# Modulation weights with outputs on partitions: one multiply-accumulate on VectorE per 128 outputs

## The chip, the cores and the metric

The kernel runs on one core of one Trainium2 chip. The metric is the device time of one execution in microseconds (us). The kernel before has a median of 2834.01 us over three runs, which lie between 2828.8 and 2840.16.

## What is computed

An encoder trunk of two layers over 256 tokens of 2048 features, in f32. A layer is a token mixer and an MLP of width 8192, and both are modulated by a condition vector `c` of 2048 numbers. Mixer 0 is a sparse attention: an indexer scores the keys, the 64 best of each query are kept, and 16 heads attend to them. Mixer 1 is RWKV-7, a recurrence over the tokens. Cut to what matters here:

```python
c_act = silu(c)                                   # [1, 2048]
for i in range(2):
    mod = c_act @ ada_w[i] + ada_b[i]             # [1, 2048] x [2048, 12288]
    sh1, sc1, g1, sh2, sc2, g2 = split(mod, 6)    # parts 0 to 5
    y = mixer[i](rms_norm(x) * (1 + sc1) + sh1)   # 0: sparse attention, 1: RWKV-7
    x = x + g1 * y
    h = rms_norm(x) * (1 + sc2) + sh2
    x = x + g2 * (square(relu(h @ mlp_w1[i])) @ mlp_w2[i])
return rms_norm(x) * final_g
```

The change is in the line of `mod` alone: a product of one row by a matrix of 2048 x 12288, 100.7 MB a layer, two layers.

## The kernel before

Features lie on the 128 partitions and tokens along the free dimension, so a feature tile is 128 x 256, and a value of `mod` is one number per partition. Every large product is made of three TensorE products: `raw` and `more` are loaded chunks of f32 weights; ScalarE casts the high part `whi` (L87), VectorE or GpSimd subtracts it to get the low part `wlo` (L89; which of the two takes a piece goes by a fixed rotation of the phase), and L182, L183 and L184 multiply high by high, high by low, and low by high.

**Phases.** The launch runs in phases that follow each other, each with its own tiles: the first mixer (until about 455 us: the projection until about 142, low-rank norms and indexer keys until 176, indexer scores until 215, the choice of the best keys until 228, heads from 259), the first MLP (503 to 1280 us in its full loop), the projections and the scan of RWKV (until about 2090), and the second MLP (until the end). An MLP is four blocks of 2048 hidden features: 16 hidden tiles, then 16 output tiles that add to `x`, so 32 weight chunks a block, each of 128 x 2048, with 48 products.

**Modulation.** There are 2 layers x 6 parts x 4 = 48 blocks (`ada_block`) of four feature tiles, 512 outputs. A block reads 4 MB as eight loads of 512 KB into the tile `araw`, which has inputs on partitions and outputs along the free dimension, and takes four steps, one for each quarter of the 16 input tiles. A block is of one of two kinds:

- "array" (17 blocks): L215 multiplies on TensorE, with the activated `c` (tile `cact`) as a stationary operand of 32 equal columns; the four input tiles of a step go to four column groups of the array. L228 then transposes the sums from PSUM in blocks of 32 on VectorE.
- "vector" (31 blocks): L217 makes the first product on ScalarE, and L219 adds the other 15 on VectorE, each a multiply by a number per partition and an add over 128 x 512, into the tile `acc`. L228 transposes `acc`, and L233 reduces it to partial sums.

Both end alike: four tiny products on TensorE (L237) sum the partial sums into a PSUM tile `ps_j`, VectorE adds the bias (L240), and for the scales it adds 1 (L242). The result lands in `mod`, four columns a block.

**Where it stands.** Parts 1 and 0 of layer 0 (eight array blocks) are made beside the first projection, since the first mixer can't start its products without them. Parts 2, 3 and 4 of layer 0 follow beside the rest of the mixer: two steps after each of the eight indexer groups (`ADA_INDEX`), six at the choice of keys (`ADA_TOPK`), two a head (`ADA_HEAD`), where the kinds go array, array, vector. Part 5 of layer 0 and five parts of layer 1 are made in the first MLP, 0.8 steps a weight chunk (`t.rate`), and the last part at 0.2 steps a chunk, enqueued for the second MLP. A scheduler orders each engine's instructions after that, by its own estimates, and each engine then works through its queue in order. So where VectorE's step stands in its queue is fixed before the launch.

The names on VectorE in the rows below: L262 ends a norm over tokens (`sm`); L432 is the turning of queries by their positions; L562 and L564 add up the indexer's scores; L616 and L618 choose the keys; L633 adds the mask to a head's logits `lg` and takes their maximum (one instruction with an accumulator, and the reading of it), L639 and L641 scale the softmax, and then TensorE transposes it.

Of the kernel before, what the change touches and what calls it, by code (L numbers as in the profile page):

```python
# [16 lines left out]
P = 128  # L17
# [79 lines left out]
class Trunk:  # L97
    def __init__(s, ctx, tc, io):
# [11 lines left out]
        s.cact = s.fix.tile([P, NF], F32, name="cact")  # L110
# [5 lines left out]
        s.turn, s.kinds, s.ada_kind = 0, "d", "j"  # L116
# [3 lines left out]
    def phase(s, name, a, b, m, w=0, q=0, l=0, g=()):  # L120
        # the working tiles of a phase: A of 2 KB and B of 1 KB a partition, split weights in pieces, modulation
# [33 lines left out]
    # weights: a chunk of up to 2048 columns, split exactly in two parts  # L155
    def raw(s, ap, own=True):
        if not own and s.bufs["m"]:
            t = s.tp.tile([P, 1024], F32, name="araw", bufs=s.bufs["m"])
        else:
            s.raws += 1  # L160
            if s.raws % (NRAW + s.bufs["q"]) < NRAW:
                t = s.wp.tile([P, 512], F32, name="raw", bufs=NRAW)[:, :ap.shape[-1]]
            else:
                t = s.tp.tile([P, 512], F32, name="more", bufs=s.bufs["q"])[:, :ap.shape[-1]]
        s.nc.sync.dma_start(t, ap)
        return t
# [32 lines left out]
    # modulation: c_act @ ada_w, four feature tiles at a time  # L199
    def ada_block(s, layer, part, j, where):  # L200
        # where the products are made: in the array, on VectorE, or on ScalarE and GpSimd
        nc = s.nc
        blk = part * 4 + j
        array = where == "array"
        if array:
            # partial sums in the four column tiles of the array
            p = s.bank(s.ada_kind)
        acc = None if array else s.tp.tile([P, 512], F32, name="acc", bufs=1 + (s.bufs["m"] > 2))
# [1023 lines left out]
```

## Time and profile before

| | before |
|---|---|
| device time, median of 3 runs | 2834.01 us (2828.8 to 2840.16) |
| span of the profiled execution | 2835.9 us |
| TensorE products busy | 2666.8 us (94%) |
| TensorE weight loads busy | 2460.3 us (87%) |
| VectorE busy | 2009.3 us (71%) |
| ScalarE busy | 1330.1 us (47%) |
| GpSimd busy | 1252.3 us (44%) |
| moved by DMA | 621.70 MB, mean 219 GB/s |

One execution was profiled; its span is the time from its first to its last instruction, and lies 1.9 us above the median of the runs and inside their spread. Busy shares are means over all phases. In the rows further below, PE is TensorE's products, PEld its weight loads, DVE VectorE, ACT ScalarE, POOL GpSimd, SP the engine that issues most DMAs. "x" is a count of instructions. PEclk is the granted clock of TensorE as a share of its full 2.4 GHz.

### The profile page before, as it was taken

Reading aid. Unit: us, or ns where it says so; the run is one execution under the profiler, and the core shown is the slowest. Engines: PE = TensorE matmul, PEld = TensorE weight load, DVE = VectorE, ACT = ScalarE, POOL = GpSimd, SP = SyncE. Lnnn points to the kernel's source line nnn. Section 1 sums busy time; section 2 is a strip of 40 time slices with the busy share of each in tenths; the row PEclk is TensorE's granted clock in tenths of the full one; section 3 lists DMA queues with packets and bytes.
Section 4 is the critical chain, followed back from the end, with each engine's and each line's share of the span. In section 5 each row is a group of like instructions: output and inputs, shape, how many; then the busy total and the mean of one; then the engine's idle time right before and its main releaser. Section 6 shows DMA issues by size and latency. Waiting matters only on the chain. (4 is left out here: it accounts for less than half of the span.)

```text
span 2835.9 us, 65852 instructions
## 1 busy us (share of the span) xinstructions
PE 2666.8 (94%) x25132; PEld 2460.3 (87%) x25132; DVE 2009.3 (71%) x3475; ACT 1330.1 (47%) x2879; POOL 1252.3 (44%) x1121
## 2 busy tenths in 40 slices
PE   7989998899999999998989899999898999999998
PEld 4566688899999999997978788888798999999998
DVE  2276658999999999948887656766798264473653
ACT  3334345445444544446655334444445454454553
POOL 1343237445454454455665412323554444444443
PEclk9998999999999999999999879999999999999999
DMA  9987836999899899854657632333577656555563
GB/s 356 367 305 289 297 106 197 299 312 332 290 302 318 291 312 318 268 174 127 201 174 224 190 91 77 105 113 89 157 262 239 193 182 183 182 182 185 182 182 115
DMA packets 290847, 621.70 MB, mean 219 GB/s; under 512 B 32353, under 2 KB 46049, under 8 KB 290529
## 3 DMA queue, kind: packets, MB, share of 16 engines
q1 hardware_dynamic: 283616, 604.89, 66.0%
q10 hardware_dynamic: 6912, 12.59, 1.2%
q8 instruction: 197, 3.23, 0.5%
q14 instruction: 122, 0.99, 0.1%
HBM read 600.57 MB, written 16.78 MB: 218 GB/s over the span
## 5 line engine op out<-in xcount | busy, mean ns | idle before, releaser
L89 POOL TENSOR_TENSOR wlo<-raw,whi 128x512 fp32r<-128x512 f32 x364 | 515.9, 1423 | 616.5 <-ACT whi L87 439.3
L87 ACT CAST whi<-raw 128x512 fp32r<-128x512 f32 x856 | 516.4, 617 | 453.5 <-PE ps_d L183 158.7
L89 DVE TENSOR_TENSOR wlo<-raw,whi 128x512 fp32r<-128x512 f32 x492 | 412.5, 842 | 236.2 <-ACT whi L87 226.4
L219 DVE SCALAR_TENSOR_TENSOR acc<-araw,cact,acc 128x512 f32<-128x512 f32 x465 | 476.2, 1025 | 8.1 <-ACT acc L217 4.4
L89 POOL TENSOR_TENSOR wlo<-more,whi 128x512 fp32r<-128x512 f32 x181 | 256.0, 1416 | 312.8 <-ACT whi L87 201.2
L87 ACT CAST whi<-more 128x512 fp32r<-128x512 f32 x366 | 223.2, 617 | 218.6 <-PE ps_d L183 75.5
L182 PE MATMUL ps_d<-A,whi 128*128 128x256 f32 x1058 | 312.7, 297 | 12.4 <-ACT B L849 4.6
L183 PE MATMUL ps_d<-A,whi 128*128 128x256 f32 x1058 | 306.1, 290 | 5.7 <-DVE A L196 5.1
L184 PE MATMUL ps_d<-A,wlo 128*128 128x256 f32 x1058 | 303.8, 287 | 0.0
L89 DVE TENSOR_TENSOR wlo<-more,whi 128x512 fp32r<-128x512 f32 (+1 forms) x185 | 152.1, 824 | 141.9 <-ACT whi L87 139.3
L182 PEld LDWEIGHTS ps_d<-A,whi 128*128 128x128 f32 x1058 | 206.0, 195 | 33.3 <-issue 6.5
L183 PEld LDWEIGHTS ps_d<-A,whi 128*128 128x128 f32 x1058 | 206.9, 196 | 10.4 <-DVE A L196 9.0
L184 PEld LDWEIGHTS ps_d<-A,wlo 128*128 128x128 f32 x1058 | 206.5, 195 | 1.4 <-issue 1.4
L183 PE MATMUL ps_d<-h,whi 128*128 128x258 f32 x552 | 157.9, 286 | 2.9 <-DVE h L352 2.8
L184 PE MATMUL ps_d<-h,wlo 128*128 128x258 f32 x552 | 156.8, 284 | 1.9 <-DVE wlo L89 1.9
L182 PE MATMUL ps_d<-h,whi 128*128 128x258 f32 x552 | 157.7, 286 | 0.0
L371 ACT ACTIVATE B<-B,sm 128x256 f32<-128x256 f32 x128 | 65.0, 508 | 197.1 <-DVE B L370 197.0
L182 PE MATMUL ps_m<-h,whi 128*128 128x258 f32 x536 | 153.2, 286 | 0.0
L183 PE MATMUL ps_m<-h,whi 128*128 128x258 f32 x536 | 152.6, 285 | 0.0
L184 PE MATMUL ps_m<-h,wlo 128*128 128x258 f32 x536 | 151.6, 283 | 0.0
L182 PE MATMUL ps_m<-A,whi 128*128 128x256 f32 x510 | 145.6, 286 | 5.4 <-DVE B L372 4.4
L183 PE MATMUL ps_m<-A,whi 128*128 128x256 f32 x510 | 145.0, 284 | 1.5 <-DVE A L375 1.5
(555 smaller groups left out, 8753.1 us busy)
## 6 DMA issues: line engine op xcount, KB each, us to landing
araw<-ada_w_in SPq DMA_DIRECT2D x384, 512.0 KB, 6.3
raw<-mlp_w_in SPq DMA_DIRECT2D x614, 256.0 KB, 4.0
more<-mlp_w_in SPq DMA_DIRECT2D x410, 256.0 KB, 4.2
raw<-b_w_r_in SPq DMA_DIRECT2D x64, 256.0 KB, 3.6
raw<-b_w_k_in SPq DMA_DIRECT2D x64, 256.0 KB, 4.0
raw<-b_w_v_in SPq DMA_DIRECT2D x64, 256.0 KB, 3.7
raw<-b_w_o_in SPq DMA_DIRECT2D x64, 256.0 KB, 3.5
hd<-A ACTq DMA_DIRECT2D x48, 256.0 KB, 4.7
```

Of the source, the lines that this page charges most:

```text
L87: t.nc.scalar.copy(hi[:, :n], r)
L89: e.tensor_tensor(lo[:, :n], r, hi[:, :n].bitcast(F32), op=OP.subtract)
L182: mm(out, wh, m[:, :w], start=i == 0, stop=False)
L183: mm(out, wh, m[:, w:], start=False, stop=False)
L184: mm(out, wl, m[:, :w], start=False, stop=i == n - 1)
L219: nc.vector.scalar_tensor_tensor(acc, wk, c, acc, op0=OP.mult, op1=OP.add)
L371: nc.scalar.activation(r, u, AF.Relu, bias=c)
```

## The change

The weights of the modulation are laid out ahead of the launch the other way round: an output tile is 128 outputs on partitions by all 2048 inputs along the free dimension, 1 MB. The activated `c` is then needed along the free dimension in every partition: a new function `spread_c` loads `c` into all 128 partitions (tile `cb`, 1 MB), ScalarE takes the sigmoid, and VectorE multiplies. It is called at the head of the first mixer and of both MLPs. A block of four output tiles now loads four tiles `araw` of 1 MB, one a step, and for each VectorE runs one instruction (L212) that multiplies the tile by `cb`, writes the product over the tile and sums it into one number a partition, which is the output. The bias is added at the end of a block, and the 1 with it (L218, L220).

L215, L217, L219, L228, L233, L237, L240 and L242 go, with the tiles `acc`, `act` and `cact`; all 48 blocks are of the one kind. The number of steps, the phases in which they are enqueued and their rates stay. The buffers of `araw` go from 9, 4 and 4 of 512 KB to 4, 2 and 2 of 1 MB. The bytes of weights are the same. Line numbers fall by about 25: L633 of before is L608, L432 is L407, L562 and L564 are L537 and L539, L262 is L240, L182 to L184 are L178 to L180.

```diff
-    # modulation: c_act @ ada_w, four feature tiles at a time
-    def ada_block(s, layer, part, j, where):
+    def spread_c(s):
+        nc = s.nc
+        s.cb = s.tp.tile([P, D], F32, name="cb", bufs=1)
+        nc.sync.dma_start(s.cb, s.io["c"].partition_broadcast(P))
+        sg = s.tp.tile([P, D], F32, name="araw", bufs=s.bufs["m"])
+        nc.scalar.activation(sg, s.cb, AF.Sigmoid)
+        nc.vector.tensor_tensor(s.cb, s.cb, sg, op=OP.mult)
+
+    def ada_block(s, layer, part, j):
         nc = s.nc
...
-        for q in range(4):
-            w = [s.raw(s.io["ada_w"][layer, blk, q, :, i * 1024:(i + 1) * 1024], False) for i in range(2)]
-            for k in range(4):
...
-        for c in range(4):
-            nc.tensor.matmul(p[c * 32:c * 32 + 32, :4], s.cv("i32"), t[:, c, :], start=True, stop=True)
...
+        acc = s.small(4)
+        for k in range(4):
+            w = s.tp.tile([P, D], F32, name="araw", bufs=s.bufs["m"])
+            nc.sync.dma_start(w, s.io["ada_w"][layer, o + k])
+            nc.vector.tensor_tensor_reduce(out=w, in0=w, in1=s.cb, scale=1.0, scalar=0.0, op0=OP.mult, op1=OP.add,
+                                           accum_out=acc[:, k:k + 1])
+            if k < 3:
                 yield
+        dst, b = s.mod[layer][:, o:o + 4], s.v(f"ada_b{layer}", o, 4)
+        if part in (1, 4):
+            nc.vector.scalar_tensor_tensor(dst, acc, 1.0, b, op0=OP.add, op1=OP.add)
         else:
+            nc.vector.tensor_tensor(dst, acc, b, op=OP.add)
         yield
...
-                s.adaq.append(s.ada_block(0, part, j, "array"))
+                s.adaq.append(s.ada_block(0, part, j))
...
-        with t.phase("dsa", a=27, b=17, m=9, q=MORE, g=(1, 2)):
+        with t.phase("dsa", a=27, b=17, m=4, q=MORE, g=(1, 2)):
+            t.spread_c()
             t.dsa()
...
-        with t.phase("mlp0", a=14, b=12, w=2, m=4, q=MORE, g=(2, 3)):
+        with t.phase("mlp0", a=14, b=12, w=2, m=2, q=MORE, g=(2, 3)):
+            t.spread_c()
...
-        with t.phase("mlp1", a=14, b=12, w=2, m=4, q=MORE, g=(2, 3)):
+        with t.phase("mlp1", a=14, b=12, w=2, m=2, q=MORE, g=(2, 3)):
+            t.spread_c()
...
-    a["ada_w"] = ct(g["ada_w"].reshape(2, 4, 4, P, 24, 512).transpose(0, 4, 1, 3, 2, 5)).reshape(2, 24, 4, P, 2048)
+    a["ada_w"] = ct(g["ada_w"].transpose(0, 2, 1)).reshape(2, 96, P, D)
+    a["c"] = ct(g["c"].reshape(-1))
```

The scheduler's order moves with it. The first place is the start of VectorE's queue. Before:

```order
L329 TENSOR_TENSOR cact<-sm,vec 128x16
L452 CAST B<-B 128x256
L89 TENSOR_TENSOR wlo<-raw,whi 128x512
L89 TENSOR_TENSOR wlo<-raw,whi 128x256
L89 TENSOR_TENSOR wlo<-raw,whi 128x512
L262 TENSOR_SCALAR sm<-ps_m 128x2
L89 TENSOR_TENSOR wlo<-more,whi 128x256
L228 STREAM_TRANSPOSE act<-ps_j 128x512
```

In the changed kernel VectorE's queue starts like this (an "ISA" row of L212 with `cb` is the new instruction, the one behind it the reading of its accumulator):

```order
L427 CAST B<-B 128x256
L203 TENSOR_TENSOR cb<-cb,araw 128x2048
L89 TENSOR_TENSOR wlo<-raw,whi 128x512
L89 TENSOR_TENSOR wlo<-raw,whi 128x256
L89 TENSOR_TENSOR wlo<-raw,whi 128x512
L240 TENSOR_SCALAR sm<-ps_m 128x2
L89 TENSOR_TENSOR wlo<-more,whi 128x256
L212 ISA araw,sm<-araw,cb 128x2048
L212 ISA sm 128x1
L212 ISA araw,sm<-araw,cb 128x2048
L212 ISA sm 128x1
```

The first new instruction stands behind the norm over tokens (L262, now L240), where the transpose of the first array block stood.

The second place is VectorE beside the indexer's scores. Before, with steps of a vector block between them:

```order
L432 TENSOR_TENSOR B<-ps_m,B 128x256
L562 TENSOR_SCALAR A<-lg,widx 128x128
L562 TENSOR_SCALAR A<-lg,widx 128x256
L219 SCALAR_TENSOR_TENSOR acc<-araw,cact,acc 128x512
L564 SCALAR_TENSOR_TENSOR A<-lg,widx,A 128x128
L564 SCALAR_TENSOR_TENSOR A<-lg,widx,A 128x256
L219 SCALAR_TENSOR_TENSOR acc<-araw,cact,acc 128x512
L564 SCALAR_TENSOR_TENSOR A<-lg,widx,A 128x128
L564 SCALAR_TENSOR_TENSOR A<-lg,widx,A 128x256
```

In the changed kernel, on the same engine at the same place:

```order
L537 TENSOR_SCALAR A<-lg,widx 128x128
L537 TENSOR_SCALAR A<-lg,widx 128x256
L212 ISA araw,sm<-araw,cb 128x2048
L212 ISA sm 128x1
L407 TENSOR_TENSOR B<-ps_m,B 128x256
L539 SCALAR_TENSOR_TENSOR A<-lg,widx,A 128x128
L212 ISA araw,sm<-araw,cb 128x2048
L212 ISA sm 128x1
L539 SCALAR_TENSOR_TENSOR A<-lg,widx,A 128x256
L212 ISA araw,sm<-araw,cb 128x2048
L212 ISA sm 128x1
L539 SCALAR_TENSOR_TENSOR A<-lg,widx,A 128x128
```

Eighteen of the new instructions stand from the first turning of queries (L407) to the choice of the keys; most of what they replace there were array blocks, which left VectorE a transpose each. In this order TensorE has the queries and keys of the first four heads ahead of the first softmax's logits, beside the indexer.

The third place is VectorE in the heads, around the softmax of the second head. Before:

```order
L635 TENSOR_SCALAR sm<-sm 128x2
L639 RECIPROCAL sm<-sm 128x2
L233 TENSOR_REDUCE sm<-act 128x16
L641 TENSOR_SCALAR lg<-lg,sm 128x128
L641 TENSOR_SCALAR lg<-lg,sm 128x256
L196 TENSOR_TENSOR A<-B,A 128x256
```

In the changed kernel (L614 is the reciprocal and L616 the scaling):

```order
L610 TENSOR_SCALAR sm<-sm 128x2
L614 RECIPROCAL sm<-sm 128x2
L212 ISA araw,sm<-araw,cb 128x2048
L212 ISA sm 128x1
L212 ISA araw,sm<-araw,cb 128x2048
L212 ISA sm 128x1
L212 ISA araw,sm<-araw,cb 128x2048
L212 ISA sm 128x1
L616 TENSOR_SCALAR lg<-lg,sm 128x128
L627 COPY B<-ps_a 128x256
L616 TENSOR_SCALAR lg<-lg,sm 128x256
L212 ISA araw,sm<-araw,cb 128x2048
```

There are six such groups of four among the 16 heads, 24 new instructions.

## Rows read from the trace of the kernel before

**Rows 1.** The page's first part: busy us, share, instructions by engine.

```profile
PE 2666.8 (94%) x25132; PEld 2460.3 (87%) x25132; DVE 2009.3 (71%) x3475; ACT 1330.1 (47%) x2879; POOL 1252.3 (44%) x1121
```

**Rows 2.** Stretches, first mixer: us, busy PE/PEld/DVE/ACT/POOL, PEclk, DMA share, GB/s.

```profile
0.00:142.00 142.00, 115.09 (x722) 65.86 (x723) 37.45 (x84) 48.53 (x97) 37.14 (x40) 0.99 0.98 362
142.00:176.00 34.00, 30.13 (x228) 21.70 (x227) 17.64 (x42) 11.05 (x28) 8.29 (x8) 0.95 1.00 358
176.00:215.00 39.00, 34.30 (x235) 22.27 (x235) 34.99 (x61) 17.57 (x38) 23.16 (x21) 0.96 0.73 264
215.00:260.00 45.00, 42.49 (x283) 31.68 (x278) 36.99 (x86) 19.21 (x41) 19.83 (x17) 0.97 1.03 395
260.00:455.00 195.00, 190.66 (x1299) 151.17 (x1298) 113.58 (x284) 76.84 (x193) 61.21 (x47) 0.95 0.55 178
```

**Rows 3.** Stretches: the first MLP's four blocks, two blocks of the second.

```profile
503.00:1280.00 777.00, 739.44 (x6130) 733.95 (x6130) 721.58 (x932) 372.96 (x738) 382.21 (x259) 0.98 0.88 291
2274.00:2644.00 370.00, 370.00 (x3094) 369.54 (x3093) 191.61 (x263) 185.62 (x352) 165.63 (x128) 1.00 0.59 182
```

**Rows 4.** TensorE's waits, 455 to 1280 us: sum, times, longest.

```profile
PE ps_j L237 <- DVE sm L233: 30.3, 10, 5.0
```

**Rows 5.** Timeline of TensorE at 733 us: start, duration, instruction, idle before.

```profile
732.93 0.29 PE L237 MATMUL ps_j<-sm,cst 128*32 128x4 f32 x8 [4.33 <-DVE sm L233]
733.14 0.58 PE L184 MATMUL ps_d<-h,wlo 128*128 128x258 f32 x1
```

**Rows 6.** Stretches of L215 alone: PE and PEld busy.

```profile
0.00:455.00 455.00, 105.14 (x544) 17.93 (x544) 0.97 0.78 278
260.00:455.00 195.00, 24.43 (x128) 4.23 (x128) 0.95 0.55 178
```

**Rows 7.** Timeline of TensorE at 86 us.

```profile
85.97 1.05 PE L215 MATMUL ps_j<-araw,cact 128*32 128x512 f32 x4
86.95 0.39 PE L476 MATMUL ps_d<-A,wlo 128*128 128x256 f32 x1
```

**Rows 8.** Timeline of VectorE at 259 us.

```profile
259.36 0.29 DVE L633 CUSTOM_DVE_ANT_0 lg<-ps_m,A 128x128 f32<-128x128 f32 x1 [1.75 <-PE ps_m L628]
259.58 0.42 DVE L633 CUSTOM_DVE_ANT_0 lg<-ps_m,A 128x256 f32<-128x256 f32 x1
259.92 0.08 DVE L633 DVE_READ_ACCUMULATOR2_ANT sm<- 128x1 f32 x1
```

**Rows 9.** Line 89 by engine: count, ns min/median/max, first to last start, forms.

```profile
L89 DVE TENSOR_TENSOR wlo<-raw,whi x492: 426/691/1784, 28.9 to 2799.7; 128x512 fp32r<-128x512 f32 x162, 128x256 fp32r<-128x256 f32 x2
L89 POOL TENSOR_TENSOR wlo<-raw,whi x364: 1262/1296/2108, 29.7 to 2801.0; 128x512 fp32r<-128x512 f32 x182
```

**Rows 10.** The tile acc, the same columns.

```profile
L219 DVE SCALAR_TENSOR_TENSOR acc<-araw,cact,acc x465: 702/747/1865, 166.9 to 2197.8; 128x512 f32<-128x512 f32 x155
```

**Rows 11.** VectorE's groups, 11 to 455 us: busy us, mean ns, idle before.

```profile
L219 DVE SCALAR_TENSOR_TENSOR acc<-araw,cact,acc 128x512 f32<-128x512 f32 x45 | 44.0, 977 | 3.0 <-ACT acc L217 2.6
...
L228 DVE STREAM_TRANSPOSE act<-ps_j 128x512 f32<-128x512 f32 x17 | 12.2, 715 | 35.7 <-PE ps_j L215 35.7
```

**Rows 12.** VectorE's groups, 455 to 1280 us.

```profile
L219 DVE SCALAR_TENSOR_TENSOR acc<-araw,cact,acc 128x512 f32<-128x512 f32 x360 | 370.0, 1028 | 4.6 <-ACT acc L217 1.8
...
L228 DVE STREAM_TRANSPOSE act<-acc 128x512 f32<-128x512 f32 x24 | 16.9, 703 | 0.3
```

**Rows 13.** Timeline of VectorE at 33 us.

```profile
32.83 0.15 DVE L262 TENSOR_SCALAR sm<-ps_m 128x2 f32<-128x2 f32 x1
```

**Rows 14.** Timeline of VectorE at 228 us.

```profile
228.39 0.36 DVE L618 TENSOR_SCALAR A<-A 128x384 f32<-128x384 f32 x1
```

**Rows 15.** The page's DMA issues: count, KB each, median us to landing.

```profile
araw<-ada_w_in SPq DMA_DIRECT2D x384, 512.0 KB, 6.3
```

**Rows 16.** The page's costliest groups: ScalarE's casts.

```profile
L87 ACT CAST whi<-raw 128x512 fp32r<-128x512 f32 x856 | 516.4, 617 | 453.5 <-PE ps_d L183 158.7
```

**Rows 17.** GpSimd's groups, 455 to 1280 us.

```profile
L89 POOL TENSOR_TENSOR wlo<-raw,whi 128x512 fp32r<-128x512 f32 x154 | 232.1, 1513 | 201.4 <-ACT whi L87 162.6 <-DMA more<-mlp_w_in 12.1 <-DVE A L375 8.7
```

More of the change, by code (lines that the diff above doesn't have):

```diff
@@ L51 @@
 for _n, _w in (
-    [("c", 16), ("final_g", 16)] + [(f"mu{i}", 16) for i in range(6)]
+    [("final_g", 16)] + [(f"mu{i}", 16) for i in range(6)]
     + [(n, 16) for n in ("w0", "a0", "k_k", "k_a", "gn_g", "gn_b", "r_k")]
@@ L115, in __init__ @@
         s.flip = s.raws = s.pieces = 0
-        s.turn, s.kinds, s.ada_kind = 0, "d", "j"
+        s.turn, s.kinds = 0, "d"
         s.due = s.rate = 0.0
@@ L153, in m, with raw @@
         return s.mod[layer][:, part * 16 + i:part * 16 + i + 1]
-    def raw(s, ap, own=True):
-        if not own and s.bufs["m"]:
-            t = s.tp.tile([P, 1024], F32, name="araw", bufs=s.bufs["m"])
-        else:
[L160 to L164, printed above, removed]
+    def raw(s, ap):
+        s.raws += 1
+        if s.raws % (NRAW + s.bufs["q"]) < NRAW:
+            t = s.wp.tile([P, 512], F32, name="raw", bufs=NRAW)[:, :ap.shape[-1]]
+        else:
+            t = s.tp.tile([P, 512], F32, name="more", bufs=s.bufs["q"])[:, :ap.shape[-1]]
         s.nc.sync.dma_start(t, ap)
@@ L197, in split @@
         return t
-    def ada_block(s, layer, part, j, where):
+    def spread_c(s):
         nc = s.nc
[L203 to L208, printed above, removed]
-        for q in range(4):
-            w = [s.raw(s.io["ada_w"][layer, blk, q, :, i * 1024:(i + 1) * 1024], False) for i in range(2)]
-            for k in range(4):
-                c = s.cact[:, q * 4 + k:q * 4 + k + 1]
-                wk = w[k // 2][:, k % 2 * 512:k % 2 * 512 + 512]
-                if array:
-                    nc.tensor.matmul(p[k * 32:k * 32 + 32, :], c.to_broadcast([P, 32]), wk, start=q == 0, stop=q == 3)
-                elif q == 0 and k == 0:
-                    nc.scalar.activation(acc, wk, AF.Copy, scale=c)
-                elif where == "vector":
-                    nc.vector.scalar_tensor_tensor(acc, wk, c, acc, op0=OP.mult, op1=OP.add)
-                else:
-                    t = s.A()
-                    nc.scalar.activation(t, wk, AF.Copy, scale=c)
-                    nc.gpsimd.tensor_tensor(acc, acc, t, op=OP.add)
-            if q < 3:
@@ new lines, in spread_c @@
+        s.cb = s.tp.tile([P, D], F32, name="cb", bufs=1)
[5 more added lines that the diff above has]
+        nc = s.nc
+        o = part * 16 + j * 4
+        acc = s.small(4)
[5 more added lines that the diff above has]
+            if k < 3:
@@ L225, in ada_block @@
                 yield
-        t = s.tp.tile([P, 512], F32, name="act", bufs=1)
-        nc.vector.transpose(t, p if array else acc)
-        if array:
-            t = t.rearrange("p (f c i)->p c f i", c=4, i=32)[:, :, :, 0]
-        else:
-            r = s.small(16)
-            nc.vector.tensor_reduce(r, t.rearrange("p (b i)->p b i", i=32), axis=AX.X, op=OP.add)
-            t = r.rearrange("p (f c)->p c f", c=4)
-        p = s.bank(s.ada_kind)
-        for c in range(4):
-            nc.tensor.matmul(p[c * 32:c * 32 + 32, :4], s.cv("i32"), t[:, c, :], start=True, stop=True)
@@ L238, in ada_block @@
-        o = part * 16 + j * 4
-        dst = s.mod[layer][:, o:o + 4]
-        nc.vector.tensor_tensor(dst, p[:, :4], s.v(f"ada_b{layer}", o, 4), op=OP.add)
-        if part in (1, 4):
-            nc.vector.tensor_scalar(dst, dst, 1.0, None, op0=OP.add)
+        dst, b = s.mod[layer][:, o:o + 4], s.v(f"ada_b{layer}", o, 4)
+        if part in (1, 4):
+            nc.vector.scalar_tensor_tensor(dst, acc, 1.0, b, op0=OP.add, op1=OP.add)
+        else:
+            nc.vector.tensor_tensor(dst, acc, b, op=OP.add)
@@ L243, in ada_block, with ada_enqueue @@
         yield
-    def ada_enqueue(s, layer, parts, where=("vector",)):
+    def ada_enqueue(s, layer, parts):
         for p in parts:
             for j in range(4):
-                s.adaq.append(s.ada_block(layer, p, j, where[j % len(where)]))
+                s.adaq.append(s.ada_block(layer, p, j))
     def ada(s, n=1):
@@ L326, in start @@
             nc.sync.dma_start(s.x[i], io["x"][:, i * S:(i + 1) * S])
-        sg = s.small(16)
-        nc.scalar.activation(sg, s.v("c", 0, 16), AF.Sigmoid)
-        nc.vector.tensor_tensor(s.cact, sg, s.v("c", 0, 16), op=OP.mult)
     def ada_due(s):
@@ L490, in dsa @@
             raw.append(t)
-        s.ada_enqueue(0, [2, 3, 4], ("array", "array", "vector"))
+        s.ada_enqueue(0, [2, 3, 4])
         def lowrank(raw, n, gname):
@@ L1173, in layout @@
     mu = g["b_mu"][0]
[L1174 removed]
+    vs = dict(final_g=g["final_g"], w0=g["b_w0"], a0=g["b_a0"], k_k=g["b_k_k"], k_a=g["b_k_a"],
               gn_g=g["b_gn_g"], gn_b=g["b_gn_b"], r_k=g["b_r_k"], q_norm_g=g["a_q_norm_g"],
```

3 lines of the change are left out of this document (removed).

## The prediction

> **What bounds the kernel now.** I read the page's busy line first, then the stretches, then TensorE's waits inside each, then the groups of the lines that the change touches. TensorE is busy for 94% of the span and VectorE for 71% [rows 1], but that is a mean over stages. The stretches of the first mixer [rows 2] show TensorE in the lead: 412.7 us of 455 over the five, against 240.7 for VectorE. Only from 176 to 260 us is VectorE nearly full too (34.99 of 39, then 36.99 of 45), and DMA stands at a share of 0.98 to 1.00 until 176 us.
>
> In the first MLP both engines are full: of 777 us, TensorE is busy 739.4 and VectorE 721.6. The same loop in the second MLP, in two of its four blocks with hardly any modulation beside it, has TensorE busy for all of 370 us, so 185 us a block, with VectorE at half [rows 3]. Four blocks at 185 would be 740, so the first MLP loses 37 us. TensorE's own waits say to whom: 30.3 us of ten waits are L237, the little products that end a modulation block, waiting for VectorE's partial sums [rows 4]. After such a wait of 4.33 us the next matmul takes 0.58 us [rows 5], and the granted clock of the stretch is 0.98, not the 1.00 of the second MLP [rows 3]. So the products of the modulation cost TensorE far more by what they wait for than by their length.
>
> **The change, part by part.**
>
> *TensorE, array products.* L215 leaves: 105.1 us busy in the first mixer, 24.4 of it from 260 us on [rows 6]. A lone pair of products (four records) holds the engine from 85.97 to 86.95 us [rows 7], so the time is real. L237 leaves as well.
>
> *One new VectorE instruction.* Its length at 2048 columns is in no row. The same form at 128 and 256 columns takes 0.29 and 0.42 us, plus 0.08 for reading the accumulator [rows 8]; 0.13 per 128 columns gives 0.42 + 14 x 0.13 + 0.08 = 2.3 us. A plain two-input subtraction takes 0.43 us at 256 columns and 0.69 at 512 [rows 9], which gives 0.43 + 7 x 0.26 + 0.08 = 2.3 too. Those are lengths without company. The old multiply-add has 0.70 as its shortest, but 0.98 as its mean in the first mixer, 1.03 in the first MLP, 1.87 at most [rows 10 to 12]: about 0.3 us of waiting for each, longest where GpSimd works. Either an instruction waits once, whatever its length (2.3 + 0.3 = 2.6), or the wait grows with the length (2.3 x 1.4 = 3.2). I take 2.6, because the longest excess, 1.16, is about one GpSimd subtraction of 1.3 [rows 9] and not a share of anything, and keep 3.2 for the range. The Trainium skill (SBUF — State Buffer, section Who interferes with whom) says that a VectorE instruction with two SBUF inputs and a GpSimd instruction that reads SBUF exclude each other for the whole of the one that started first; by that rule the 2.6 stands, and without it the sum below would be 48 us worse on VectorE in the first mixer.
>
> *First mixer, VectorE's total.* Away: 44.0 us of multiply-adds and 12.2 for 17 transposes [rows 11], some 4 for the other reductions. Added: 80 x 2.6 = 208. So 240.7 - 60 + 208 = 389 of 455, while TensorE falls to 412.7 - 105 - 3 = 305. The bound changes hands; the question is in which stage.
>
> *Until 142 us.* In the changed order the first new instruction stands behind the token norm's VectorE step, now at 32.8 us [rows 13]. From there VectorE has its other work of this stretch, 34 us (37.5 less some 3 done before), less 6 of transposes, and 32 x 2.6 = 83: it ends at about 33 + 28 + 83 = 144. Behind the last sum lie a normalisation, two activations and the last 84 products at 0.12 (the 185 us of a full block by its 32 weights of 48 products), some 11 us, of which 2 us are counted already: 153. **+11**. TensorE and DMA are not late here: 51 MB have moved by 142 us (142 x 362 GB/s), where 32 MB of modulation and about 10 of the rest are needed.
>
> *142 to 215 us, the indexer.* The chain before the first rope keeps its 34 us, to 187. The stage after it, 39 us with VectorE busy 34.99, loses about 10 of multiply-adds and transposes, and takes 18 new instructions (47 us) and some 7 weight subtractions that come forward (5): 35 - 10 + 47 + 5 = 77, ending at 264 instead of 215. VectorE is the bound of it.
>
> *To the first softmax.* The top-k keeps its 14 us (215 to 228.4, [rows 14]): 278. Before, the first softmax started only at 259.36 [rows 8], since TensorE still had the queries and keys to do, and one vector block ran; in the new order TensorE does that work beside the indexer. So 49 us late becomes **+19** in all.
>
> *260 to 455 us, the heads.* TensorE's 190.7 less 24.4 and about 1.5 for L237 is 165; VectorE's 113.6 less 18 plus 24 x 2.6 is 158. From 278, 165 us lead to 443. But the 24 new instructions stand in six groups of four, 10.4 us each: three (once all four) ahead of the scaling of every second head, for which TensorE's transposes wait, the fourth behind it, ahead of the next head's maximum. TensorE has other products queued there; I charge 2.5 us a group: 458. The first mixer ends **3 us later** than before. Bounds: 30 us earlier if VectorE idles only where it must (33 + 389, with little after it), 48 later if each group is paid in full.
>
> *First MLP.* VectorE loses 370.0 and 16.9 of transposes [rows 12] and about 16 of reductions, and gains 96 x 2.7 = 259 (307 at 3.2): 721.6 falls to 577 or 626 of 740. TensorE no longer waits for any sum. I keep 3 us of the 37 for the waits on hidden tiles: **-34**. Bounds: -37 and 0.
>
> *The new operand.* Its load is 1 MB written, twice a block of 512 KB that lands in 6.3 us [rows 15]; its sigmoid is four casts of 0.62 [rows 16], its product one more 2.3. At the start all of it lies before 33 us. At the head of each MLP a table load and these stand in ScalarE's and VectorE's queues: between 0 and 10 us a time. For the first MLP I take 3. In the second, 60 multiply-adds at 1.03 become 16 at 2.7, 19 us off VectorE, against the same setup: 0.
>
> Sum against the profiled execution: 3 - 34 + 3 = -28 on 2835.9, so 2808. That span is 1.9 us above the median of the runs, inside their spread of 11: 2807.
>
> **Rivals.**
>
> *VectorE's groups of four decide the heads (slower).* If TensorE's fixed order has nothing ready while a head waits, each of six groups costs its whole 10.4 us: 278 + 165 + 62 = 505, 50 later than before. With -34 and +3: 2853. For it: VectorE is an in-order queue and fuller than TensorE until 278. Against: output products and the next block's queries stand between the heads. It turns the sign once the groups cost over 43 us together. 0.17.
>
> *The first MLP keeps its loss.* GpSimd's subtractions take 1.51 us there [rows 17] against 1.3 alone [rows 9]. Two GpSimd and two VectorE subtractions a weight, 0.8 new instructions of 2.3 and the two-input steps on hidden tiles come to about 2.6 + 1.3 + 1.8 + 0.3 = 6.0 us of exclusive reads a weight, against 5.8 of TensorE. If reads bind, -34 becomes about 0: 2841. Against: VectorE's waits would have to fall on TensorE, which now shows none on weights above 2.5 us. 0.14.
>
> *TensorE's relief shows.* The first mixer at its bound of -30: 2774. 0.12.
>
> *The change does not do what it says.* If summing needs two passes a column, 4.3 us more than doubles the new work: 80 x 2 = 160 more where VectorE binds, and nothing gained in the MLP: about 2970. Against: the maximum form runs at a column a cycle's pace [rows 8]. 0.05.
>
> **Numbers.** The forecast, 2807, has 0.50, with 2788 to 2826 as its own range from the bounds above; 0.02 is left to what I don't see. The range 2770 to 2850 takes in the forecast, TensorE's relief and the unchanged MLP, and cuts the slow rivals. A measurement here tells 0.5% (14 us) from no change. Faster: 0.45 of the forecast and 0.12. Same: 0.05, 0.14 and 0.07 of the first rival. Slower: 0.10 of it, 0.05, 0.02.
>
> **What would show it.** Right: new instructions near 2.6 us; no PE wait on sums in the first MLP, its four blocks near 743 and clock at 1.00; first softmax at 275 to 285; VectorE the fullest engine until then. Wrong: lengths over 3.2, PE waits on a head's scaled logits of tens of us, or blocks still at 200.

## The result and the profile after

The changed kernel takes 2857.75 us in the median of four runs (2852.55 to 2867.09), the kernel before 2832.52 beside it: a ratio of 1.0095, with a 95% interval of 1.0067 to 1.0122. It is slower by just under 1%, above the range of 2770 to 2850. The profiled execution has a span of 2857.6 us, 21.7 more than before.

The page's first part of the changed kernel answers to [rows 1]:

```profile
PE 2576.9 (90%) x24204; PEld 2455.4 (86%) x24204; DVE 2078.9 (73%) x3301; ACT 1310.6 (46%) x2851; POOL 1372.2 (48%) x1121
```

TensorE lost 90 us of work and VectorE gained 70. GpSimd gained 120 us with not one instruction more.

Where the 21.7 us come from is read from the same steps in both traces: the last product of the projection, the end of the choice of keys (L618, now L593), the first maximum of a head (L633, L608), the first squared hidden tile of the first MLP (L372, L347), and the last output of each MLP.

| us | before | after | difference of the stage |
|---|---|---|---|
| end of the projection | 142.7 | 157.1 | +14.4 |
| keys chosen | 228.4 | 290.6 | +47.8 |
| first maximum of a head | 259.4 | 291.1 | -30.5 |
| first MLP begins | 505.6 | 556.9 | +19.6 |
| first MLP ends | 1282.6 | 1321.6 | -12.3 |
| second MLP begins | 2092.7 | 2114.7 | -17.0 |
| second MLP ends | 2822.3 | 2844.5 | +0.2 |

The 30 us won back before the first maximum are TensorE's queries and keys, which the new order has beside the indexer. Each row comes from one profiled execution. So the first mixer is 51.3 us longer (forecast: 3), the first MLP 12 us shorter (forecast: 31 with the setup of `cb`), RWKV's phases 17 shorter (forecast: 0), the second MLP as long as before (forecast: 0).

The stretches of the first mixer in the changed kernel, cut at these steps, answer to [rows 2] (columns as there):

```profile
0.00:157.00 157.00, 64.90 (x403) 62.72 (x404) 116.23 (x136) 49.26 (x99) 57.00 (x40) 0.88 0.92 338
157.00:196.00 39.00, 26.65 (x160) 24.02 (x158) 26.49 (x45) 12.40 (x30) 12.20 (x9) 0.78 0.54 190
196.00:275.00 79.00, 61.31 (x339) 49.85 (x340) 78.57 (x92) 30.41 (x67) 53.15 (x32) 0.83 0.86 310
275.00:291.00 16.00, 12.54 (x51) 8.80 (x50) 15.88 (x60) 4.68 (x11) 9.10 (x7) 0.73 0.65 222
291.00:507.00 216.00, 173.46 (x1098) 151.72 (x1098) 149.78 (x309) 74.79 (x187) 62.34 (x44) 0.84 0.52 179
```

Beside the indexer VectorE is busy for 78.57 of 79 us: it is the bound there. Among the heads neither engine is full, VectorE with 149.8 and TensorE with 173.5 of 216, and the granted clock is 0.84, a mean over stretches at its two levels of 1.2 and 2.4 GHz.

The new instruction in the page's costliest groups (count, busy us, mean ns, idle before):

```profile
L212 DVE CUSTOM_DVE_ANT_0 araw<-araw,cb 128x2048 f32<-128x2048 f32 x192 | 497.3, 2606 | 5.0 <-DMA araw<-ada_w_in 4.9
```

In the answer on its line (ns shortest/median/longest), and in the one on line 89, GpSimd's subtraction, which answers to [rows 9]:

```profile
L212 DVE CUSTOM_DVE_ANT_0 araw<-araw,cb x192: 2270/2284/3389, 34.0 to 2395.4; 128x2048 f32<-128x2048 f32 x192
```

```profile
L89 POOL TENSOR_TENSOR wlo<-raw,whi x364: 1257/1296/3397, 25.1 to 2823.5; 128x512 fp32r<-128x512 f32 x182
```

2.28 us alone and 2.61 as a mean: the two numbers of the forecast (2.3 and 2.6). What was mis-sized is not the instruction but who waits behind it.

The three later phases, after (first MLP, RWKV, second MLP) and then before:

```profile
556.90:1321.60 764.70, 732.46 (x5978) 729.42 (x5976) 647.16 (x718) 354.65 (x716) 448.42 (x260) 0.98 0.85 298
1321.60:2114.70 793.10, 736.66 (x9888) 663.54 (x9889) 574.50 (x1331) 390.01 (x967) 340.70 (x412) 0.94 0.45 143
2114.70:2844.50 729.80, 724.91 (x6011) 724.21 (x6009) 418.26 (x535) 363.89 (x713) 349.42 (x261) 1.00 0.61 195
```

```profile
505.60:1282.60 777.00, 739.10 (x6127) 733.52 (x6125) 719.40 (x929) 371.85 (x736) 382.21 (x259) 0.98 0.88 290
1282.60:2092.70 810.10, 748.34 (x9940) 672.71 (x9941) 586.43 (x1351) 390.85 (x971) 350.69 (x414) 0.94 0.49 144
2092.70:2822.30 729.60, 721.89 (x5990) 719.85 (x5988) 405.67 (x552) 364.33 (x712) 332.79 (x259) 0.99 0.61 189
```

In the first MLP VectorE fell from 719 to 647 us, and yet the clock stayed at 0.98 and TensorE kept 32 us of idle time. Its waits there (sum, times, longest) name other releasers than [rows 4]:

```profile
PE ps_b L178 <- ACT A L349: 12.7, 3, 5.7
PE ps_m L178 <- ACT A L349: 6.4, 2, 5.6
PE ps_d L179 <- DVE A L350: 6.2, 2, 3.4
```

L349 and L350 write the hidden tiles. The waits on partial sums are gone, as forecast; TensorE now waits at the change from hidden to output tiles of a block.

### The profile page after: what moved, and what is told of

Same layout as the page of the kernel before. It is cut to its first block, busy times and chain, and to the rows that moved or that the text cites. A ratio compares the mean times of both kernels' runs of the same rounds, so it can differ in the third digit from the quotient of the medians.

```text
span 2857.6 us, 63201 instructions
## 1 busy us (share of the span) xinstructions
PE 2576.9 (90%) x24204; PEld 2455.4 (86%) x24204; DVE 2078.9 (73%) x3301; ACT 1310.6 (46%) x2851; POOL 1372.2 (48%) x1121
## 4 chain that ended last, share of the span: by engine, by line
PE 70%; DVE 7%; issue 4%; DMA 2%; POOL 2%; ACT 1%; SPq 0%; DVEq 0%; POOLq 0%; ACTq 0%
PE ps_d L178 9%; PE ps_d L179 9%; PE ps_d L180 9%; PE ps_m L179 5%; PE ps_m L178 5%; PE ps_m L180 5%; PE ps_b L179 3%; PE ps_b L178 3%; PE ps_b L180 3%; PE ps_a L178 3%; PE ps_a L179 3%; PE ps_a L180 3%; DVE araw L212 2%; PE ps_m L882 1%; DVE wlo L89 1%
## 5 line engine op out<-in xcount | busy, mean ns | idle before, releaser
L89 POOL TENSOR_TENSOR wlo<-raw,whi 128x512 fp32r<-128x512 f32 x364 | 575.5, 1589 | 577.0 <-ACT whi L87 451.4
L212 DVE CUSTOM_DVE_ANT_0 araw<-araw,cb 128x2048 f32<-128x2048 f32 x192 | 497.3, 2606 | 5.0 <-DMA araw<-ada_w_in 4.9
L89 POOL TENSOR_TENSOR wlo<-more,whi 128x512 fp32r<-128x512 f32 x181 | 271.3, 1502 | 319.8 <-ACT whi L87 205.0
L178 PE MATMUL ps_d<-A,whi 128*128 128x256 f32 x1058 | 317.3, 302 | 21.3 <-DVE x L370 9.0
L179 PE MATMUL ps_d<-A,whi 128*128 128x256 f32 x1058 | 312.3, 296 | 11.8 <-DVE A L350 6.2
L180 PE MATMUL ps_d<-A,wlo 128*128 128x256 f32 x1058 | 310.8, 294 | 0.6 <-DVE wlo L89 0.4
L89 DVE TENSOR_TENSOR wlo<-more,whi 128x512 fp32r<-128x512 f32 (+1 forms) x185 | 164.6, 892 | 133.4 <-ACT whi L87 130.4
L178 PEld LDWEIGHTS ps_d<-A,whi 128*128 128x128 f32 x1058 | 213.2, 202 | 31.8 <-DVE x L370 10.8
L179 PEld LDWEIGHTS ps_d<-A,whi 128*128 128x128 f32 x1058 | 214.4, 203 | 15.7 <-DVE A L192 8.2
L180 PEld LDWEIGHTS ps_d<-A,wlo 128*128 128x128 f32 x1058 | 214.2, 202 | 1.7 <-DVE wlo L89 1.2
L178 PE MATMUL ps_d<-h,whi 128*128 128x258 f32 x552 | 157.4, 285 | 0.0
L180 PE MATMUL ps_d<-h,wlo 128*128 128x258 f32 x552 | 156.3, 283 | 0.9 <-DVE wlo L89 0.9
L178 PE MATMUL ps_m<-A,whi 128*128 128x256 f32 x510 | 146.9, 288 | 8.3 <-ACT A L349 8.3
L347 DVE TENSOR_TENSOR B<-B 128x256 f32<-128x256 f32 x128 | 111.1, 868 | 59.0 <-ACT B L346 59.0
L178 PE MATMUL ps_m<-h,whi 128*128 128x258 f32 x536 | 152.3, 284 | 0.0
L180 PE MATMUL ps_m<-h,wlo 128*128 128x258 f32 x536 | 151.0, 282 | 0.0
```

What stands on the lines that cost most here:

```text
L89: e.tensor_tensor(lo[:, :n], r, hi[:, :n].bitcast(F32), op=OP.subtract)
L178: mm(out, wh, m[:, :w], start=i == 0, stop=False)
L179: mm(out, wh, m[:, w:], start=False, stop=False)
L180: mm(out, wl, m[:, :w], start=False, stop=i == n - 1)
L212: nc.vector.tensor_tensor_reduce(out=w, in0=w, in1=s.cb, scale=1.0, scalar=0.0, op0=OP.mult, op1=OP.add, accum_out=acc[:, k:k + 1])
L347: nc.vector.tensor_tensor(q, r, r, op=OP.mult)
```

## The experiments

All ratios are against the kernel before, run on the same chip. "Mixer" is the time at which the first MLP begins; this and the two columns behind it are read from one profiled execution of each kernel. That execution is the slowest of six in e12 (2813.11 us) and the fastest of four in e9 (2794.56).

| run | median us | ratio (95%) | mixer | first MLP | RWKV |
|---|---|---|---|---|---|
| changed kernel | 2857.75 | 1.0095 (1.0067 to 1.0122) | 556.9 | 764.7 | 793.1 |
| e1_mixer_old | 2811.3 | 0.9904 (0.9881 to 0.9926) | 498.2 | 762.7 | 805.4 |
| e2_mlp_old | 2883.69 | 1.0166 (1.0145 to 1.0187) | 557.8 | 776.8 | 803.6 |
| e3_dummy | 2849.85 | 1.0050 (1.0033 to 1.0067) | 553.5 | 762.7 | 791.6 |
| e4_drop | 2777.8 | 0.9786 (0.9755 to 0.9818) | 470.7 | 762.1 | 802.7 |
| e5_mlp_split | 2827.57 | 0.9975 (0.9962 to 0.9989) | 505.9 | 770.7 | 806.0 |
| e6_mlp_drop | 2765.67 | 0.9768 (0.9741 to 0.9795) | 499.9 | 716.0 | 806.1 |
| e7_head_drop | 2820.13 | 0.9949 (0.9932 to 0.9966) | 508.8 | 762.9 | 804.9 |
| e8_split_all | 2888.88 | 1.0196 (1.0179 to 1.0213) | 571.2 | 768.6 | 795.8 |
| e9_rates | 2808.21 | 0.9895 (0.9861 to 0.9928) | 494.3 | 758.8 | 797.7 |
| e10_before_rates | 2853.61 | 1.0064 (1.0041 to 1.0086) | 500.1 | 779.6 | 827.4 |
| e11_after_rates | 2859.01 | 1.0080 (1.0053 to 1.0107) | 550.0 | 761.6 | 796.7 |
| e12_rates_mid | 2797.18 | 0.9857 (0.9826 to 0.9887) | 506.8 | 751.1 | 809.4 |

What a difference in these columns is worth can be read from kernels with the same code in a phase. The mixer of e1, e5, e6, e9 and e12, the old one, ends between 494 and 507 us; the new one, in the changed kernel, e2 and e11, between 550 and 558. The first MLP with the plain new sums takes 762 to 765 us (the changed kernel, e1, e3, e4, e7).

### The change in one phase at a time: e1 and e2

Both forms stand in one kernel, with a copy of the weights in each layout. In e1 the mixer has the old blocks (20 blocks, 17 array and 3 vector; the "9 vector" in the expectation is a slip), in e2 the MLPs have.

```diff
-                s.adaq.append(s.ada_block(0, part, j))
+                s.adaq.append(s.ada_block_old(0, part, j, "array"))
...
-        s.ada_enqueue(0, [2, 3, 4])
+        s.ada_enqueue(0, [2, 3, 4], ("array", "array", "vector"))
```

> The first mixer goes back to the old modulation (17 array and 9 vector blocks... all of its 20 blocks as before), both MLPs keep the new instruction. In the changed kernel the first MLP's first block starts 51 us late (556.9 against 505.6 us), the first MLP takes 12 us less, RWKV's phases 17 us less, the second MLP the same. If these belong to their own phases, the start is back at 503 to 510 us and the sum is 2836 - 29 = 2807 (2800 to 2814). If the 17 us of RWKV's phases came from the mixer's part of the change (another order of the whole), they are gone and it takes 2823 (2816 to 2830).

> The reverse: the new instruction in the first mixer alone, both MLPs with the old vector blocks. If the gains belong to the MLPs' part of the change: start of the first MLP's first block at 550 to 560 us, its four blocks back at 777, RWKV's phases back at 810, in all 2836 + 51 = 2887 (2880 to 2895). If RWKV's 17 us belong to the mixer's part: 2870.

The loss is the mixer's: with its old blocks the first MLP begins at 498.2 us, with the new sums at 557.8. The first MLP's gain of 12 to 14 us is its own (762.7 against 776.8). RWKV's 17 us come back with neither part alone: 805 and 804, where the kernel before has 810 and the changed kernel 793. e1 is 1% faster than the kernel before; some 7 of its 27 us are its mixer, whose blocks are the old ones, and which ends within the spread given above.

### VectorE's sums or TensorE's clock: e3 and e4

e3 gives TensorE as many products as the change took away, each behind the sum just made. e4 leaves 48 sums out.

```diff
+            if extra:
+                for q in range(4):
+                    nc.tensor.matmul(p[q * 32:q * 32 + 32, :], acc[:, k:k + 1].to_broadcast([P, 32]), s.cb[:, q * 512:q * 512 + 512], start=k == 0, stop=k == 3)
```

> The changed kernel with 272 products more on TensorE in the first mixer, as many and as long as the array products that the change removed (moving tile: the spread c, stationary: the sum just made), written to a PSUM tile that nothing reads. VectorE's work is the same. Theory V (VectorE's queue makes the mixer late, and the low granted clock of 0.66 to 0.89 there only goes along with it): first MLP's first block within 8 us of 557 or later, 2850 to 2880 in all, though the granted clock rises. Theory C (the removed products had kept the clock up, and the slower products on the path make most of the 51 us): granted clock over 0.92 from 100 to 450 us, first block at 515 to 540, 2820 to 2840.

```diff
+            if layer == 0 and part in (2, 3, 4):
+                nc.vector.tensor_copy(acc[:, k:k + 1], w[:, 0:1])
+            else:
```

> The changed kernel without the sums of parts 2, 3 and 4 of layer 0: their weights are loaded, and VectorE copies one column of each tile in place of the sum, so 48 of the 80 new instructions of the first mixer are left out and these modulation values are not computed. TensorE gets nothing back. Theory V: the projection ends at 157 us as in the changed kernel, the rest runs as before or better, first block at 500 to 515, 2800 to 2816. Theory C: the clock stays low without products to fill TensorE, first block at 525 to 545, 2826 to 2846.

e3 moved the mixer's end by 3 us, and e4 by 86. Theory V holds, but e4 overshot it: it ends the mixer 35 us sooner than the kernel before. That is not the worth of the array products alone. e4 also lacks the old vector blocks (44.0 us of multiply-adds on VectorE [rows 11]) and their transposes, and has the new order of the queues; its 35 us are not divided among these. e3 is not a clean test of the clock. In the projection its products wait for the sums, and the granted clock did not rise; here are the changed kernel from 50 to 157 us, and e3 from 50 to 155:

```profile
50.00:157.00 107.00, 49.87 (x335) 48.06 (x336) 94.91 (x106) 36.78 (x72) 48.75 (x31) 0.82 0.91 337
```

```profile
50.00:155.00 105.00, 84.79 (x554) 48.74 (x555) 95.09 (x106) 37.28 (x73) 49.28 (x31) 0.82 0.91 343
```

TensorE is 85 us busy instead of 50 at the same clock of 0.82, and the stage ends 2 us sooner: VectorE, busy 95 us in both, sets it.

Among the heads the added products did raise the clock. From 291 to 477 us, the changed kernel and then e3:

```profile
291.00:477.00 186.00, 143.52 (x854) 122.12 (x854) 129.91 (x269) 62.34 (x161) 45.26 (x33) 0.81 0.53 184
```

```profile
291.00:477.00 186.00, 157.40 (x1029) 122.17 (x1028) 135.88 (x279) 64.76 (x169) 48.48 (x36) 0.91 0.56 189
```

At 0.91 instead of 0.81 the last maximum of a head starts at 473.2 us, in the changed kernel at 477.1. So the clock came up and the heads' loss stayed. The 128 added products took 19 us of TensorE's own time there, so what a higher clock would give without them is not shown.

### The heads: e7

e7 keeps all sums but the last 24, which stand among the heads (same edit as e4, for part 4 and half of part 3).

> The changed kernel with the last 24 of the first mixer's sums left out in the same way, those that stand among the heads; the other 56 stay. If the groups of four ahead of a head's scaling are paid nearly in full (rival: 62 us), the first maximum stays at 291 us and the first MLP's first block comes at 500 to 515, 50 us sooner than in the changed kernel: 2800 to 2815 in all. If TensorE has other products to fill the waits, as forecast (15 us): 535 to 545, 2837 to 2846.

The first maximum stays at 291.0, the first MLP begins 48 us sooner. So the six groups cost 48 of their 62 us, 8 each and not the 2.5 that I charged. The median, 2820.13, lies 5 us above the range expected. VectorE around one group in the changed kernel (start, duration, instruction, idle before), from the reciprocal to the scaling:

```profile
302.21 0.17 DVE L614 RECIPROCAL sm<-sm 128x2 f32<-128x2 f32 x1 [1.43 <-ACT lg L612]
302.29 2.27 DVE L212 CUSTOM_DVE_ANT_0 araw<-araw,cb 128x2048 f32<-128x2048 f32 x1
...
304.49 2.29 DVE L212 CUSTOM_DVE_ANT_0 araw<-araw,cb 128x2048 f32<-128x2048 f32 x1
...
306.70 2.29 DVE L212 CUSTOM_DVE_ANT_0 araw<-araw,cb 128x2048 f32<-128x2048 f32 x1
...
308.91 0.28 DVE L616 TENSOR_SCALAR lg<-lg,sm 128x128 f32<-128x128 f32 x1
```

And TensorE at the same place, with the transposes of the head before and of this one:

```profile
299.91 0.87 PE L619 MATMUL ps_b<-cst,lg 128*128 128x128 f32 x3 [1.66 <-DVE lg L616]
...
309.34 1.20 PE L619 MATMUL ps_b<-cst,lg 128*128 128x128 f32 x3 [2.90 <-DVE lg L616]
```

The scaling is ready to run at 302.4 and runs at 308.9. TensorE has products for a part of that time, then waits 2.90 us, and its next three transposes take 1.20 instead of 0.87. Both show in the sums over the heads: the changed kernel's longest waits there, then the same stretch of e7, which answers to the last of the changed kernel's five stretches above.

```profile
PE ps_b L619 <- DVE lg L616: 28.5, 9, 7.0
PE ps_d L178 <- DVE x L370: 9.0, 4, 4.7
```

```profile
291.00:459.00 168.00, 161.19 (x1096) 143.63 (x1096) 99.82 (x286) 74.40 (x187) 60.34 (x48) 0.93 0.64 232
```

The same products (1098 and 1096 records) take 173.5 us with the sums at a clock of 0.84 and 161.2 without them at 0.93. TensorE is idle for 42.5 of 216 us, against 6.8 of 168. Of the 48 us, then, 36 are idle time and 12 are products that took longer. This divides the time; it does not show that the clock alone would give back the 12, and in e3 a higher clock brought the last maximum only 4 us forward.

### What the first MLP still loses: e5, e6 and e8

e6 leaves out the first MLP's 96 sums and keeps their loads; e5 cuts each sum of the MLPs in four; both have the old mixer. e8 is the changed kernel with every sum cut.

```diff
+            for q in range(4):
+                wq = w[:, q * 512:q * 512 + 512]
+                nc.vector.tensor_tensor_reduce(out=wq, in0=wq, in1=s.cb[:, q * 512:q * 512 + 512], scale=1.0, scalar=0.0,
+                                               op0=OP.mult, op1=OP.add, accum_out=acc[:, k * 4 + q:k * 4 + q + 1])
```

> The first mixer as before, the MLPs with the new sums, each cut into four of 512 columns whose results a small reduction adds at the end of a block. With whole sums of 2.3 to 3.4 us the first MLP took 762.7 us (740 would be four blocks of 185), and TensorE's longest waits there are 5.6 to 5.7 us on the last hidden tiles of a block, which stand behind such sums on VectorE. Theory G (the grain: one long instruction holds up the short steps on hidden tiles): first MLP 745 to 755, in all 2795 to 2803. Theory B (VectorE's total, or the memory ports, bound it): 760 to 770, since pieces cost more in all, 2808 to 2818.

> The first mixer as before; in the first MLP the 96 sums are left out (the weights are loaded, one column is copied in place of each sum, so the modulation made there is not computed). This gives the floor. If the sums are what still costs the first MLP 22 us: 740 to 746 and 2786 to 2795 in all. If the loads of modulation weights beside the MLP's own cost it (310 GB/s there): 755 to 763 still, 2803 to 2812.

> The changed kernel with every sum cut into four of 512 columns, in the first mixer too. If the mixer's 51 us come from VectorE's total and from the order of its queue, cutting changes little or makes it worse: first block at 550 to 570; with a gain of 0 to 15 in the first MLP 2840 to 2870 in all. If the length of the single instruction is what holds the heads up: first block at 515 to 535, 2805 to 2830.

The floor is 716, lower than all I had expected: with all the loads TensorE is busy for 715.6 of 716 us (the last line further below), so the loads cost nothing there. The sums cost 47 us in e1 (762.7 - 716.0) where the old blocks had cost 61 (777.0 - 716.0). Cutting them lost 8 us in the MLP, and 14 in the mixer, so grain is not it. Both kernels came out slower than either theory had allowed, e5 by 10 us and e8 by 19; 8 of e5's are its mixer, with the same code as e1's. A piece, from the answer on e5's line:

```profile
L215 DVE CUSTOM_DVE_ANT_0 araw<-araw,cb x448: 675/681/1814, 491.4 to 2371.9; 128x512 f32<-128x512 f32 x150
```

Four pieces are 2.72 us against 2.28 for a whole.

Do the engines' waits for each other, at the memory ports, make the 47 us? Line 89 in the first MLP on VectorE and GpSimd (ns shortest/median/longest), e1 and then e6:

```profile
L89 DVE TENSOR_TENSOR wlo<-raw,whi x153: 674/685/1798, 502.3 to 1256.7; 128x512 fp32r<-128x512 f32 x153
L89 POOL TENSOR_TENSOR wlo<-raw,whi x146: 1277/1552/3396, 501.5 to 1246.7; 128x512 fp32r<-128x512 f32 x146
```

```profile
L89 DVE TENSOR_TENSOR wlo<-raw,whi x153: 677/691/1780, 504.6 to 1211.7; 128x512 fp32r<-128x512 f32 x153
L89 POOL TENSOR_TENSOR wlo<-raw,whi x147: 1284/1295/1778, 500.4 to 1201.7; 128x512 fp32r<-128x512 f32 x147
```

Beside the sums GpSimd's subtractions are longer (3.40 us at most, in e5 beside the pieces 1.85), and in all it is busy for 444 us of e1's first MLP, 382 of e5's and 330 of e6's. But e5, which gave some 60 of these back, took 8 us more. So the hold on GpSimd does not set the phase. VectorE's share is different: it is busy for 642 us in e1, 709 in e5 and 377 in e6, in the order of the times. How much of its 642 us is waiting for GpSimd is not resolved.

Where VectorE's load counts is seen by halves of a block, hidden tiles and output tiles, cut at VectorE's steps on hidden tiles. Second block in e1, then in e6 with the whole first MLP as its last line:

```profile
682.92:780.46 97.54, 91.69 (x734) 90.98 (x733) 89.91 (x101) 46.80 (x106) 52.80 (x31) 0.96 0.84 287
780.46:875.65 95.19, 95.19 (x785) 95.19 (x785) 71.82 (x83) 41.32 (x68) 59.06 (x34) 0.99 0.96 333
```

```profile
669.44:756.22 86.78, 86.78 (x722) 86.78 (x722) 61.98 (x91) 49.75 (x106) 38.74 (x31) 1.00 0.88 314
756.22:854.17 97.95, 97.95 (x818) 97.95 (x818) 34.09 (x69) 43.02 (x71) 44.02 (x35) 1.00 0.91 332
499.90:1215.90 716.00, 715.64 (x5952) 715.55 (x5950) 376.89 (x623) 369.57 (x719) 330.19 (x260) 1.00 0.89 319
```

VectorE has 62 us of its own work in a hidden half and 34 in an output half. With the sums spread evenly it is 92% busy in the hidden half, which takes 97.5 us instead of 86.8, and 75% in the output half, which loses nothing. Over all four blocks the hidden halves take 390 us in e1 and 333 in e6, the output halves 373 and 383.

### Moving the sums to the output halves: e9, e10, e11 and e12

```diff
-                s.ada_due()
+                s.ada_due(0.375 if layer == 0 else 1.0)
...
-                s.ada_due()
+                s.ada_due(1.625 if layer == 0 else 1.0)
```

These are the factors of e9, e10 and e11, on a rate of 0.8; e12 has 0.6875 and 1.3125.

> The first mixer as before, the new sums in the MLPs, and in the first MLP 0.3 steps of modulation a weight chunk in the hidden halves of a block and 1.3 in the output halves, where it was 0.8 in both (in VectorE's order 6 to 9 sums a hidden half instead of 11 to 14). With 0.8 the hidden halves took 89 to 104 us with VectorE 0.91 to 0.94 busy, where 72 to 88 is the floor without sums; the output halves stood at their floor with VectorE at 0.75. Theory H (VectorE in the hidden halves is what the first MLP still loses): hidden halves 75 to 94, first MLP 725 to 742, 2772 to 2792 in all. Theory B (the total of sums beside GpSimd binds, wherever they stand): first MLP 757 to 767, 2804 to 2816.

> The kernel before with the same rates of 0.3 and 1.3, as a control: its vector blocks keep VectorE at 0.96 to 1.00 in both halves, so nothing is to be had: theory H 2828 to 2842 (first MLP 770 to 785). If moving the steps pays by itself, whatever the form: 2795 to 2815.

> The changed kernel with the same rates, the new sums in the first mixer too. Theory H: the mixer's 51 us stay, the first MLP gets to 725 to 742, in all 2820 to 2838. Theory B: 2850 to 2862.

> As the run with rates of 0.3 and 1.3 and the first mixer as before, with 0.55 and 1.05 (in VectorE's order 7 to 12 sums a hidden half, 11 to 15 an output half). At 0.3 and 1.3 the hidden halves came to their floor, but two of the output halves took 123 us with the DMA at a share of 0.98 and 349 GB/s, so the first MLP stayed at 759. If both limits are real (VectorE in the hidden halves, the loads in the output halves), a place between them does better: first MLP 735 to 752, 2780 to 2800 in all. If the sums cost the same wherever they stand: 757 to 765, 2803 to 2815.

e9 gained 4 us in the MLP, not 25 or more; e11 3 us. Their medians lie in the ranges of theory B, so by the time theory H failed: a sum moved to an output half cost nearly as much there. In e9 the hidden halves came down to 322 us in all from e1's 390, but the output halves rose from 373 to 437. The lost time had moved, as the output half of the first block and the hidden half behind it show:

```profile
577.31:700.62 123.31, 118.97 (x988) 118.59 (x987) 96.72 (x90) 58.02 (x109) 74.04 (x42) 1.00 0.98 347
700.62:775.50 74.88, 69.28 (x559) 68.68 (x557) 69.24 (x86) 36.60 (x84) 39.24 (x22) 0.96 0.78 270
```

The first of these holds 988 records of products where e6's has 818: VectorE came late to the next half, and TensorE was already in it. So my reading of its DMA share of 0.98, in the expectation of e12, falls: TensorE was busy for 118.97 of 123.31 us and did not wait for loads. e12, with rates between those of e1 and e9, came nearest, 751 us in the first MLP, at the edge of what was expected. By its median it is the fastest version that leaves nothing out: 1.4% less than before. Its runs spread from 2788 to 2813, and its lead on e1 and e9, whose intervals overlap its own, is not shown. e10 was the control: the old vector blocks gain nothing from the move, since VectorE is full with them in both halves (in the kernel before it is busy for 96 to 100% of every half but the last, which has few of them left).

e10 showed one thing more. Its RWKV phases take 827 us, 17 more than in the kernel before, whose code there is the same; the scheduler wrote VectorE's queue in another order. That is no chance of one execution: e10's four lie within 3 us of each other. This put its median 12 us above the range expected. Over all runs the phase lies between 792 and 827 us: 792 to 798 in the kernels with every new sum in mixer and MLPs and in e9, 803 to 809 in the others that have some of the new sums, 810 and 827 in the two that have none.

## Why the prediction was wrong

- **The instruction: right.** 2.3 alone and 2.6 in company were forecast, 2.28 and 2.61 measured. The choice between one wait per instruction and a wait in proportion was right too: the longest is 3.39, one of GpSimd's 1.3 more at most. The rule of the Trainium skill (SBUF — State Buffer, section Who interferes with whom), that the one that started first holds the other off for all of its length, agrees from the other side: GpSimd's subtraction has 1.30 as its median and 3.40 as its longest, about one new instruction more; before, the longest was 2.11 [rows 9].
- **Until 142 us: right.** +11 forecast, +14 measured. VectorE sets the stage (e3).
- **The indexer: right in kind, 13 us short.** VectorE is full for 79 us where I had 77. Missing were 4 us of the projection, and 6 in the step behind it: the prediction says that "the chain before the first rope keeps its 34 us", but it holds new sums as well and took 40 (157.1 to 197.1, the first product of the scores). The choice of keys took 2 more. Keys were chosen at 290.6, not at 278.
- **The heads: the step that failed.** "TensorE has other products queued there; I charge 2.5 us a group." e7 measured 8 a group, 48 in all. The forecast for this stage was 16 us less than before, and it came out 20 longer. The first rival had named the place and the price (62 us), and put the sum at 2853; it was the right case, with a chance of 0.17. That its sum came within 5 us is luck: against it the groups cost 14 us less, the indexer 13 more, the first MLP 19 more and RWKV's phases 17 less. TensorE did have other products, but in the group shown they lasted only until 306.4 (309.34 less the wait of 2.90), 4 us into it. What no rival had is that 12 of the 48 us are products that took longer, at a lower granted clock. e3, with the clock up and the loss still there, speaks against the clock as the main cause.
- **First MLP: mis-sized.** -34 forecast (-31 with the setup), -12 measured. The waits on sums went as forecast, but "I keep 3 us of the 37" took the loss to go with them; the new sums still cost 47 us (e1 and e6), and the loss passed to waits on hidden tiles. I had VectorE's load as a mean over 777 us ("721.6 falls to 577 or 626 of 740"). It fell to 647: the sums came to 254 us as forecast (259), but VectorE's remaining work to 393, where 331 are left of the 722 before without the old blocks' own. In part this is arithmetic, since the rows' durations overlap with those of the next instruction, by 0.07 to 0.08 us in [rows 8]; the rest is open. This work is unequal, 62 us in a hidden half and 34 in an output half, and the sums still fill the hidden halves; moving them to the output halves moved the loss (e9). The floor, 740 by four blocks at 185 us, is 716. The second rival had foreseen that the loss stays, by the memory ports; most of it stayed. That GpSimd is held off does not make it (e5); what VectorE's own waits at the ports add is open.
- **The other rivals.** TensorE's relief did not show in the changed kernel; e4, which leaves 48 sums out, ends the mixer 35 us sooner than before, but not by TensorE's relief alone. Two passes a column fell: 2.28 us.
- **RWKV's 17 us: open.** The forecast has nothing for them. Neither the mixer's nor the MLPs' new sums bring them alone (e1, e2), and a mere move of steps elsewhere costs 17 the other way (e10). That the order of the queues does it was not tried by itself.
- **Two slips in its sums.** 2808 less 1.9 is 2806, not 2807; and the bound "48 later" for the mixer is the rival's "50 later" (505 against 455).

## What to carry to other kernels

A sum that one engine makes in one long instruction is priced by what stands behind it in that engine's queue, in the narrowest stage: the 24 sums among the heads cost 48 us (e7). Against the old form the stage with the 32 beside the projection is 14 us longer, and the second MLP as long as before. Take an engine's load by the halves of a loop, not by its mean: a hidden half at 92% loses time beside an output half at 75%. But moving work to the emptier half won back at most 12 of 47 us here (e9, e12). The same edit can be split by phase: the new form pays in the first MLP and loses in the mixer, and the mixed kernel is 1 to 1.4% faster than before.

## What the runs showed of the hardware

- GpSimd's busy time rose from 1252 to 1372 us with the same 1121 instructions, because the long two-input sums on VectorE hold its subtractions off: with every sum cut in four (e8) it is 1256 again, on e8's page. A busy share can be waiting time.

```profile
PE 2578.6 (89%) x24204; PEld 2455.8 (85%) x24204; DVE 2164.7 (75%) x4501; ACT 1306.4 (45%) x2851; POOL 1255.7 (44%) x1121
```

- TensorE's granted clock stands at 0.73 to 0.88 in the five stretches of the first mixer, where it was 0.95 to 0.99 [rows 2]. TensorE is idle there for 20 to 59% of a stretch; among the heads the same products took 173.5 us at 0.84 and 161.2 at 0.93. Products added to fill its idle time there raised the clock from 0.81 to 0.91 (e3) and brought the last maximum 4 us forward.
- One sum over 2048 columns takes 2.28 us, four over 512 take 2.72: (2.72 - 2.28) / 3, about 0.15 us, is paid for each further instruction (medians; the reading of each accumulator, 0.08, comes on top).
